# Six attention groups as one pipeline of 24 steps, with a new group order and a combine that is fed directly

## The chip, the cores and the metric

One Trainium2 chip, one of its cores. A core has five engines with queues of their own: TensorE (PE, with its weight loads shown apart as PEld), VectorE (DVE), ScalarE (ACT), GpSimd (POOL) and SyncE (SP), which in this kernel issues nearly all DMAs. The metric is device microseconds (us) of one launch, lower is better. Times are medians of runs; the profile is that of one more execution.

## The reference

One layer of a causal decoder trunk for 1024 prompt tokens and 32 sample tokens (8 sequences of 4), width 1024, all in float32:

```python
h = layer_norm(ALPHA * x + 0.5 * swiglu(x, f1_w1, f1_w3, f1_w2), ln1_g, ln1_b)
z = h @ w_in + b_in                       # q, k, v, uv, ga, gb
# attention: 3 groups of 4 heads of 64, (window, dilation) = (128,1), (512,4), (2048,16)
s = q @ k.T * SCALE + bias                # banded by window, positions split by dilation
m = max(s); p = exp(s - m); l = sum(p); o = (p @ v) / l; lse = m + log(l)
att = sum over the 3 groups of o * softmax(lse over the groups)
yb, vrows = sgu_branch(uv, ...)           # chunked causal gating
mix = (sigmoid(ga) * (att @ w_oa) + sigmoid(gb) * (yb @ w_ob)) @ w_out
h = layer_norm(ALPHA * h + mix, ln2_g, ln2_b)
h = layer_norm(ALPHA * h + 0.5 * swiglu(h, f2_w1, f2_w3, f2_w2), ln3_g, ln3_b)
```

The sample tokens attend to stored windows; the new windows are outputs too. The change is in the prompt's attention and in the weighting of its three groups.

## The kernel before, in words

Activations lie transposed: 128 features on the partitions, 1056 tokens (1024 prompt, 32 sample) along the free axis, in four chunks of 264. Float32 products are made of three matmuls on split operands (high part times high, high times low, low times high), line L240. The kernel runs through a first feed-forward stage, the projection `z` (`widen`, which writes each block of 128 rows of z to a DRAM tensor `zD`), the stage `mix`, and a second feed-forward stage. Everything below is in `mix`.

`mix` has a foreground of dense matmuls: the remaining gate blocks of z (`dense8`; they are stored to `zD` or kept), then 32 "locals" (`local`: eight blocks of 128 output rows by four chunks, twelve matmuls of `yb @ w_ob` each, whose result is multiplied into the gate tile `mt` on DVE, line L1544), then 32 products of `att @ w_oa` with six matmuls each (the same line L1544 after them), then the product with `w_out`. Each foreground piece ends with `tick`, which advances background generators: `bg` by 2 or 3 yields (`STEPS`), `slow` by 1, `mid` by 3. In `bg` stand six `attend` generators, one for each pair of head pair `hp` (0, 1) and group `g` (0, 1, 2), in the order `HPG` = (0,0), (0,1), (0,2), (1,0), (1,1), (1,2). In `mid` stand the gating branch (`sgu_norm`, `sgu_mix`) and the `combine` of a head pair; in `slow` the attention of the sample tokens (`sample`, which streams slabs `kv` from DRAM through the "M" tiles, line L1365) and `sample_join`.

One `attend` loads q, k, v (`fetch_z`, line L1138, 528 KB each) and the bias (L1165, L1172), transposes v to `V` (L1180) and makes four steps over pairs of query blocks. A step is `scores` (eight matmuls, L1200; then on DVE the bias and the row minimum, L1208, and on ACT the exponential with its row sum, L1212), `turn` (transposes of the probabilities, L1223, copied by ACT, L1227) and `values` (L1239, copied by ACT to the group's result `aT`, L1246 or L1250). The pipeline is filled and emptied in each group: in round t come `values(t-2)`, `turn(t-1)`, `scores(t)`. At its end the row minima and sums `ml` are transposed (L1263), copied (L1265) and stored to DRAM as `mlD` (L1267).

`combine(hp)` starts when all three groups of a head pair are done. It loads `mlD` back in the tokens' own order (`raw`, L1284, L1289), computes the three groups' weights with 16 partitions on DVE (L1298 to L1311) and one exponential on ACT, stores them as `cD` (L1313), loads each weight row broadcast over 64 partitions (`cbs`, L1318, three tiles), multiplies (L1323, L1325) and adds (L1326) into a new tile `att`. `held` allocates a tile and marks it with a copy by POOL (L108). `split_att` then splits `att` into high and low parts (L251 on ACT, L252 on DVE) for the product with `w_oa`.

All larger tiles come from one pool, "S", with 37 buffers: a load into a tile waits until the last reader of the buffer's former tile is done. PSUM has three "mm" tiles for the foreground and five "ax" tiles. The instructions of all generators are put into their final order by a list scheduler that works on its own estimates of durations; the order on each engine is then fixed, and a DMA that waits holds up those behind it on SP.

Of the kernel before, what the change touches and what calls it, by code (L numbers as in the profile page):

```python
# [21 lines left out]
P = 128  # L22
# [31 lines left out]
HPG = [(hp, g) for hp in range(2) for g in range(3)]  # L54
# [9 lines left out]
SPREAD = 2  # L64
# [17 lines left out]
class Trunk:  # L82
# [1000 lines left out]
    def widen(self):  # L1083
        nc, a = self.nc, self.a
        self.att = [None, None]
        self.attT = {}
# [67 lines left out]
    def attend(self, i):  # L1154
        nc, a = self.nc, self.a
        hp, g = HPG[i]
        w, dil = GROUPS[g]
        self.fetch_qkv(i)
        q, k, v = self.qkv.pop(i)
        bias = self.M([P, 2, 256])  # L1160
        bd = self.bD[g]
        if g < 2:
            for h in range(2):
                b = bd[2 * hp + h]
                nc.sync.dma_start(bias[:, h], bass.AP(b.tensor, b.offset + 127, [[383, P], [1, 256]]))  # L1165
        else:
            nc.vector.memset(bias[:, :, :P], BIG)
            for h in range(2):
                b = bd[2 * hp + h]
                for r in range(2):  # L1170
                    o = slice(64 * r, 64 * r + 64)
                    nc.sync.dma_start(bias[o, h, o], bass.AP(b.tensor, b.offset + 255, [[383, 64], [1, 64]]))  # L1172
        yield from self.pause(2 if i else 8)
        follower = i + 1
        V = self.Q([P, 8, P])
        for b in range(2):
            p = self.ax_tile()
            for i in range(4):
                j = 4 * b + i
                nc.tensor.transpose(p[:, i * P : (i + 1) * P], v[:, j * P : (j + 1) * P], self.ident)  # L1180
            nc.scalar.copy(V[:, 4 * b : 4 * b + 4], p.rearrange("p (i x) -> p i x", i=4))
            yield
        ml = self.X([P, 2, 2, 8], "ml")
        aT = self.S([P, NP])
        self.attT[hp, g] = aT
        prob, turned, pv = {}, {}, {}

        def span(i):
# [3 lines left out]
        def scores(t):  # L1192
            s = prob[t] = self.S([P, 2, 2, 256])
            pS = [self.ax_tile().rearrange("p (r k) -> p r k", r=2) for _ in range(2)]
            for r in range(2):
                i = 2 * t + r
                nk, k0, _ = span(i)
# [5 lines left out]
            for h in range(2):  # L1203
                for r in range(2):
                    i = 2 * t + r
                    nk, _, b0 = span(i)
# [9 lines left out]
        def turn(t):  # L1216
            s = prob.pop(t)
            pT = [self.ax_tile().rearrange("p (h k) -> p h k", h=2) for _ in range(2)]
            for r in (1, 0):
                for h in range(2):  # L1220
                    for b in range(span(2 * t + r)[0] // P):
                        o = slice(b * P, b * P + P)
                        nc.tensor.transpose(pT[r][:, h, o], s[:, r, h, o], self.ident)  # L1223
            sT = turned[t] = self.S([P, 2, 2, 256])
            for r in (1, 0):
                nk = span(2 * t + r)[0]
                nc.scalar.copy(sT[:, r, :, :nk], pT[r][:, :, :nk])  # L1227

        def values(t):
            sT = turned.pop(t)  # L1230
            if t % 2 == 0:
                pv[0] = self.ax_tile()
            for r in range(2):
                i = 2 * t + r
                nb = span(i)[0] // P
# [7 lines left out]
            if t % 2:  # L1243
# [3 lines left out]
                else:  # L1247
                    n = dil // 2
                    o = aT.rearrange("p (j r) -> p r j", r=dil)[:, n * b : n * b + n, :]
                    nc.scalar.copy(o, pv[0].rearrange("p (r j) -> p r j", r=n))  # L1250
# [12 lines left out]
        nc.tensor.transpose(pm, ml.rearrange("p m h i -> p (m h i)"), self.ident)  # L1263
        mt = self.X([32, P], "mt")
# [600 lines left out]
```

## Time and profile before

| | |
|---|---|
| median of three runs | 2182.03 us (2177.48 to 2182.41) |
| the profiled execution's own time | 2182.69 us |
| its span, first to last instruction | 2180.6 us |
| PE busy | 2129.5 us, 98% of the span |
| DVE, ACT busy | 1558.7 us (71%), 891.4 us (41%) |
| HBM | 304.34 MB read, 165.60 MB written, 216 GB/s over the span |
| granted TensorE clock, mean | 0.991 |
| part of the span with prompt attention on PE | 1072.6 to 1285.6 us |

The page gives busy times of engines and, for groups of instructions, the count, the mean duration and the idle time before them with what ended it. Times within the span are counted from its start. A row of the view of busy times by stretch has the stretch, its length, then busy time and count for PE, PEld, DVE, ACT and POOL, then the granted clock of TensorE (1.00 is full speed), the busy share of the DMA engines and GB/s.

### The profile page before, as it was taken

Reading aid. Unit: us, or ns where it says so; the run is one execution under the profiler, and the core shown is the slowest. Engines: PE = TensorE matmul, PEld = TensorE weight load, DVE = VectorE, ACT = ScalarE, POOL = GpSimd, SP = SyncE. Lnnn points to the kernel's source line nnn. Section 1 sums busy time; section 2 is a strip of 40 time slices with the busy share of each in tenths; the row PEclk is TensorE's granted clock in tenths of the full one; section 3 lists DMA queues with packets and bytes.
Section 4 is the critical chain, followed back from the end, with each engine's and each line's share of the span. In section 5 each row is a group of like instructions: output and inputs, shape, how many; then the busy total and the mean of one; then the engine's idle time right before and its main releaser. Section 6 shows DMA issues by size and latency. Waiting matters only on the chain.

```text
span 2180.6 us, 43243 instructions
## 1 busy us (share of the span) xinstructions
PE 2129.5 (98%) x17305; PEld 2090.8 (96%) x17305; DVE 1558.7 (71%) x2731; ACT 891.4 (41%) x1680; POOL 326.6 (15%) x247
## 2 busy tenths in 40 slices
PE   9999999999999999999999997999999999999997
PEld 8999999999998999999998897999999999999997
DVE  8776776656798725787666558778577677657886
ACT  5444444421124734334365553255444444421224
POOL 0432332200010012232000000000333233100000
PEclk9999999999999999999999999999999999999998
DMA  4445545698874335666855645414354554597842
GB/s 159 146 135 170 190 154 166 215 346 325 327 275 163 126 106 182 208 214 229 297 170 200 192 161 179 175 67 148 120 177 158 177 177 158 181 408 274 307 183 80
DMA packets 168569, 426.57 MB, mean 196 GB/s; under 512 B 24416, under 2 KB 59984, under 8 KB 165680
## 3 DMA queue, kind: packets, MB, share of 16 engines
q1 hardware_dynamic: 167936, 423.28, 55.3%
q8 instruction: 135, 2.21, 0.4%
q10 hardware_dynamic: 432, 0.54, 0.1%
q14 instruction: 66, 0.54, 0.1%
HBM read 304.34 MB, written 165.60 MB: 216 GB/s over the span
## 4 chain that ended last, share of the span: by engine, by line
PE 83%; DMA 7%; DVE 5%; ACT 2%; issue 1%; POOL 1%; SPq 0%; ACTq 0%; DVEq 0%; POOLq 0%
PE ax L240 45%; PE mm L240 35%; DMA S<-zD 2%; DMA M<-kv 1%; DMA R<-wz 1%; PE ax L1200 1%; PE ax L1239 1%; DVE W L252 1%; DVE S L252 1%; PE ax L1223 1%; DMA S<-hD 0%; DVE S L627 0%; DMA R<-wzp 0%; DVE S L1544 0%; ACT S L251 0%
## 5 line engine op out<-in xcount | busy, mean ns | idle before, releaser
L240 PE MATMUL mm<-S,W 128*128 128x264 f32 x5208 | 693.1, 288 | 22.1 <-DVE S L1544 9.9
L240 PE MATMUL ax<-S,W 128*128 128x264 f32 x5400 | 707.2, 284 | 1.1 <-ACT S L1030 0.9
L240 PEld LDWEIGHTS mm<-S,W 128*128 128x128 f32 x5208 | 657.1, 190 | 39.5 <-issue 11.8
L240 PEld LDWEIGHTS ax<-S,W 128*128 128x128 f32 x5400 | 676.7, 188 | 3.6 <-ACT S L1030 1.9
L240 PE MATMUL ax<-S,S 128*128 128x264 f32 x3240 | 476.9, 285 | 4.6 <-DVE S L1039 3.0
L240 PEld LDWEIGHTS ax<-S,S 128*128 128x128 f32 x3240 | 428.0, 188 | 6.1 <-DVE S L1039 4.4
L240 PE MATMUL mm<-S,S 128*128 128x264 f32 x2472 | 384.9, 286 | 2.6 <-DVE S L252 2.3
L240 PEld LDWEIGHTS mm<-S,S 128*128 128x128 f32 x2472 | 335.1, 189 | 4.3 <-DVE S L252 2.5
L251 ACT CAST W<-R 128x1024 fp32r<-128x1024 f32 (+3 forms) x173 | 128.5, 761 | 301.8 <-PE mm L240 136.4
L382 POOL TENSOR_TENSOR Q<-R 128x512 f32<-128x512 f32 x49 | 70.9, 1446 | 796.9 <-DMA R<-wz 180.9
L252 DVE TENSOR_TENSOR W<-R,W 128x1024 fp32r<-128x1024 f32 (+3 forms) x173 | 155.5, 902 | 22.8 <-ACT W L251 22.2
L251 ACT CAST W<-Q 128x1024 fp32r<-128x1024 f32 (+1 forms) x78 | 76.7, 984 | 223.3 <-DVE Q L383 89.2
L816 DVE SCALAR_TENSOR_TENSOR S<-ax,S 128x264 f32<-128x264 f32 x240 | 99.5, 427 | 67.7 <-PE ax L240 67.4
L457 DVE TENSOR_TENSOR S<-ax,M 128x264 f32<-128x264 f32 x82 | 32.7, 433 | 149.3 <-PE ax L240 144.4
L252 DVE TENSOR_TENSOR S<-Q,S 128x1024 fp32r<-128x1024 f32 (+1 forms) x78 | 111.1, 1424 | 4.1 <-ACT S L251 3.8
L252 DVE TENSOR_TENSOR W<-Q,W 128x1024 fp32r<-128x1024 f32 (+1 forms) x78 | 90.5, 1160 | 24.4 <-ACT W L251 24.4
L251 ACT CAST S<-Q 128x1024 fp32r<-128x1024 f32 (+1 forms) x78 | 76.7, 984 | 68.5 <-PE ax L240 50.1
L108 POOL CAST S<-ones 128x1 fp32r<-128x1 f32 x32 | 17.5, 567 | 490.3 <-PE mm L240 308.2
L251 ACT CAST S<-R 128x512 fp32r<-128x512 f32 (+1 forms) x64 | 44.0, 687 | 107.3 <-DMA sumsA<-S 40.4
L252 DVE TENSOR_TENSOR S<-S,M 128x528 fp32r<-128x528 f32 x72 | 84.5, 1173 | 3.0 <-ACT M L251 1.4
L383 POOL TENSOR_TENSOR Q<-Q,R 128x512 f32<-128x512 f32 x49 | 81.9, 1671 | 2.7
L390 POOL TENSOR_TENSOR Q<-R,Q 128x512 f32<-128x512 f32 x49 | 80.7, 1648 | 1.1
(207 smaller groups left out, 2050.2 us busy)
## 6 DMA issues: line engine op xcount, KB each, us to landing
ws<-st SPq DMA_DIRECT2D x144, 256.0 KB
S<-sumsA SPq DMA_DIRECT2D x63, 528.0 KB
S<-sumsB SPq DMA_DIRECT2D x63, 528.0 KB
M<-kv SPq DMA_DIRECT2D x96, 256.0 KB
sumsA<-M SPq DMA_DIRECT2D x90, 264.0 KB
sumsB<-M SPq DMA_DIRECT2D x90, 264.0 KB
R<-w13b SPq DMA_DIRECT2D x44, 512.0 KB
R<-w13a SPq DMA_DIRECT2D x42, 512.0 KB
```

The costliest lines, as they stand in the source:

```text
L108: self.nc.gpsimd.tensor_copy(t[:, 0, :1] if len(shape) == 3 else t[:, :1], self.ones[:, :1])
L240: mm = lambda a, b, s, e: nc.tensor.matmul(o, a[:, cc], b, start=s, stop=e, skip_group_check=True)
L251: a = self.nc.scalar.copy(hi, src)
L252: b = self.nc.vector.tensor_tensor(lo, src, hi.bitcast(F32), op=ALU.subtract)
L382: tt(s12[:, lo], cd[:, lo], cd[:, hi], op=ALU.add)
L383: tt(s12[:, hi], s12[:, lo], ab[:, lo], op=ALU.subtract)
L390: tt(s34[:, hi], ab[:, hi], s12[:, hi], op=ALU.subtract)
L457: go(one, 5, False, lambda x: tt(h[:, x, 1], one[x], p7[:, x], op=ALU.add))
L816: nc.vector.scalar_tensor_tensor(y(x, r, e), bank[x], HALF, y(x, r, e), op0=ALU.mult, op1=ALU.add)
L1200: nc.tensor.matmul(pS[h][:, r, :nk], q[e, i * P : (i + 1) * P], k[e, k0 : k0 + nk], start=True, stop=True)
L1223: nc.tensor.transpose(pT[r][:, h, o], s[:, r, h, o], self.ident)
L1239: nc.tensor.matmul(pv[0][e, (i % 4) * P : (i % 4 + 1) * P], V[:, i - (nb - 1) + b, e], sT[:, r, h, b * P : b * P + P], start=b == 0, stop= ...
```

## The change

`HPG` becomes (0,1), (0,2), (0,0), (1,1), (1,2), (1,0); the blocks of q, k and v are projected and the sample's pairs are formed in that order too. The six generators become one, with 24 steps that run through without emptying: round n holds `scores(n)` and `turn(n-1)`, then two yields, `values(n-2)`, two yields. In the third round of a group the next group's q, k, v are loaded, in its fourth round their v is transposed (`begin`). Biases are loaded for two groups at once into one "S" tile, before in "M" tiles.

The result `att` is built in group 0's own tile, which is why group 0 comes last: groups 1 and 2 store their minima and sums as before, but load them back as soon as group 2 is done (`sums`), while group 0's are transposed straight into the layout that `combine` uses, two transposes and one copy without DRAM. `combine` starts with the arithmetic; of the three broadcast weight tiles two are loaded at first and the third when the first multiply is issued. Group 0's multiply writes in place, where before it wrote a fourth tile. `sample_join` is put ahead of the column sums in `slow`.

```diff
-HPG = [(hp, g) for hp in range(2) for g in range(3)]
+HPG = [(hp, g) for hp in range(2) for g in (1, 2, 0)]
...
-        for t in range(6):
-            if t > 1:
-                values(t - 2)
-            if 0 < t < 5:
-                turn(t - 1)
-            if t < 4:
-                scores(t)
-            if t == 3:
-                self.fetch_qkv(follower)
-            yield from self.pause(SPREAD)
-        pm = self.ax_tile()[:32, :P]
-        nc.tensor.transpose(pm, ml.rearrange("p m h i -> p (m h i)"), self.ident)
-        mt = self.X([32, P], "mt")
-        nc.vector.tensor_copy(mt, pm)
-        D_ = self.mlD[hp, g]
-        nc.sync.dma_start(D_.rearrange("m h (i x) -> (m h i) x", x=P), mt)
-        yield
-        if g == 2:
-            self.mid.append(self.combine(hp))
-            if hp:
-                self.slow.append(self.sample_join())
+        def sums(i):
+            hp, g = HPG[i]
+            ml = open_.pop(i)[3]
+            if g:
+                pm = self.ax_tile()[:32, :P]
+                nc.tensor.transpose(pm, ml.rearrange("p m h i -> p (m h i)"), self.ident)
+                mt = self.X([32, P], "mt")
+                nc.vector.tensor_copy(mt, pm)
+                nc.sync.dma_start(self.mlD[hp, g].rearrange("m h (i x) -> (m h i) x", x=P), mt)
+                if g == 1:
+                    return
+                raw = self.held([P, 3 * 2 * P])[:16].rearrange("p (g m x) -> p g m x", g=3, m=2)
+                self.raw[hp] = raw
+                for g in (1, 2):
...
+            else:
+                pm = self.ax_tile()[:16, : 2 * P].rearrange("p (m x) -> p m x", m=2)
+                for m in range(2):
+                    nc.tensor.transpose(pm[:, m], ml[:, m].rearrange("p h i -> p (h i)"), self.ident)
+                nc.vector.tensor_copy(self.raw[hp][:, 0], pm)
+                self.mid.append(self.combine(hp))
...
+        N = 4 * len(HPG)
+        for n in range(N + 2 + 1):
+            i, t = divmod(n, 4)
+            if n < N:
+                scores(n)
+            if 0 <= n - 1 < N:
+                turn(n - 1)
+            if t == 2 and i < len(HPG):
+                self.fetch_qkv(i + 1)
+                if i % 2:
+                    biases.update((x, load_bias(x)) for x in range(i + 1, min(i + 3, len(HPG))))
+            yield from self.pause(2)
+            if 0 <= n - 2 < N:
+                values(n - 2)
+                if (n - 2) % 4 == 3:
+                    sums((n - 2) // 4)
+            if t == 3 and i + 1 < len(HPG):
+                begin(i + 1)
+            yield from self.pause(2)
...
     def combine(self, hp):
-        att, *cbs = [slot([P, NT]) for _ in range(4)]
...
+        load(0)
+        load(1)
         yield from self.pause(3)
-        for g, cb in enumerate(cbs):
-            cb, aT = cb[:, :NP], self.attT.pop((hp, g))
-            if g == 0:
-                nc.vector.tensor_tensor(att[:, :NP], aT, cb, op=ALU.mult)
-            else:
-                nc.vector.tensor_tensor(aT, aT, cb, op=ALU.mult)
+        for g in range(3):
+            aT = self.attT.pop((hp, g))
+            load(g + 2)
+            nc.vector.tensor_tensor(aT, aT, cbs.popleft(), op=ALU.mult)
+            if g:
                 nc.vector.tensor_tensor(att[:, :NP], att[:, :NP], aT, op=ALU.add)
```

Since every instruction's place comes from the scheduler, the order on each engine moves. Two places follow, first before and then after; line numbers of the changed kernel are its own.

SP, the DMA queue, around the loads of q, k, v of (1,1), the blocks `zD_8631`, `zD_8637` and `zD_8643` (before L1138, after L1137). Before:

```order
L212 DMA ws<-st 16x4096 x2
L1365 DMA M_13150<-kv 128x512
L1172 DMA M_14900<-bD 64x64 x4
L1365 DMA M_13151<-kv 128x512
L1365 DMA M_13149<-kv 128x512
L1365 DMA M_13150<-kv 128x512
L1138 DMA S_14372<-zD_8631 128x1056
L1138 DMA S_14374<-zD_8637 128x1056
L1138 DMA S_14376<-zD_8643 128x1056
```

After (L1269 stores `mlD`, L1278 loads it back, L1623 stores a gate block, L218 loads a weight block, and L1137 of `zD_8648` is a tile of the gating branch):

```order
L1398 DMA M_13108<-kv 128x512
L1269 DMA mlD<-X_13813 32x128
L1137 DMA S_13848<-zD_8648 128x1056
L1278 DMA S_13816<-mlD 8x16x8 x4
L1137 DMA S_13912<-zD_8631 128x1056
L1623 DMA zD_8656<-W_13857 256x1x264
L1137 DMA S_13914<-zD_8637 128x1056
L1137 DMA S_13916<-zD_8643 128x1056
L218 DMA R_14470<-wzp 128x1024
```

Three slab loads and four bias loads no longer stand right ahead of these loads; a store and four loads of `mlD` do.

DVE, the end of `combine(1)` (multiplies L1323 and L1325 before, L1357 after; adds L1326, now L1359; the split of `att` L252, now L251; the locals' multiplies L1544, now L1577). Before:

```order
L1323 TENSOR_TENSOR S_15243<-S_14195,S_15245 128x1024
L1544 TENSOR_TENSOR S_15388<-S_15388,mm_15809 128x264
L1325 TENSOR_TENSOR S_14631<-S_14631,S_15247 128x1024
L1544 TENSOR_TENSOR S_15388<-S_15388,mm_15823 128x264
L1325 TENSOR_TENSOR S_14955<-S_14955,S_15249 128x1024
L1544 TENSOR_TENSOR S_15388<-S_15388,mm_15837 128x264
L1326 TENSOR_TENSOR S_15243<-S_15243,S_14631 128x1024
L252 TENSOR_TENSOR W_15876<-R_15875,W_15876 128x256
L1326 TENSOR_TENSOR S_15243<-S_15243,S_14955 128x1024
L252 TENSOR_TENSOR S_15870<-S_15243,S_15869 128x32
L252 TENSOR_TENSOR S_15870<-S_15243,S_15869 128x1024
L1544 TENSOR_TENSOR S_15857<-S_15857,mm_15884 128x264
```

After:

```order
L1357 TENSOR_TENSOR S_14717<-S_14717,S_15322 128x1024
L251 TENSOR_TENSOR W_15577<-R_15576,W_15577 128x512
L1577 TENSOR_TENSOR S_15228<-S_15228,mm_15582 128x264
L1466 COPY S_13968<-ax_15596 64x32 x2
L1466 COPY S_15059<-ax_15596 64x32 x2
L1359 TENSOR_TENSOR S_15059<-S_15059,S_14717 128x1024
L1577 TENSOR_TENSOR S_15228<-S_15228,mm_15606 128x264
L251 TENSOR_TENSOR S_15849<-S_13968,S_15848 128x32
L1577 TENSOR_TENSOR S_15228<-S_15228,mm_15620 128x264
L251 TENSOR_TENSOR S_15855<-S_15059,S_15854 128x32
L1577 TENSOR_TENSOR S_15228<-S_15228,mm_15634 128x264
L251 TENSOR_TENSOR S_15855<-S_15059,S_15854 128x1024
```

Before, the last local's multiply (`mm_15837`) stands ahead of the last add, and the first product with `w_oa` (`mm_15884`) right behind the split; after, the split's last row has 12 more locals' multiplies behind it (`mm_15654` to `mm_15822`) before the first product with `w_oa` (`mm_15869`).

More of the change, by code (lines that the diff above doesn't have):

```diff
@@ L63 @@
 MID = 3
-SPREAD = 2
 HOP = (4, 1, 4)
@@ L1294, in combine @@
-        yield
+        raw = self.raw.pop(hp)
+        t = [raw[:, g] for g in range(3)]
         nat = lambda g, x: x.rearrange("p (r b) -> p b r", r=GROUPS[g][1])
@@ L1563, in mix @@
         self.mid.extend(sgu)
-        self.bg.extend(self.attend(i) for i in range(len(HPG)))
-        kept, end = {}, NLEAD + NTAIL - LAST
+        self.bg.append(self.attend())
+        self.sums, kept, end = None, {}, NLEAD + NTAIL - LAST
         units = {NLEAD: self.unit(a["wzp"][NLEAD])}
```

162 lines of the change are left out of this document (86 added, 76 removed).

## The prediction

> **What bounds the kernel now.** I read the page first: PE is busy nearly all the time, so a change in the attention can only win what PE loses around it, and it can lose at most as much again as it makes PE wait.
>
> ```profile
> PE 2129.5 (98%) x17305; PEld 2090.8 (96%) x17305; DVE 1558.7 (71%) x2731; ACT 891.4 (41%) x1680; POOL 326.6 (15%) x247
> ```
>
> Busy times by stretch of the stage with the attention show where PE loses (columns: stretch, length, busy time and count of PE, PEld, DVE, ACT, POOL, then granted clock, DMA share, GB/s):
>
> ```profile
> 1060.00:1140.00 80.00, 79.46 (x677) 72.93 (x677) 55.77 (x158) 49.40 (x120) 0.00 (x0) 1.00 0.66 220
> 1140.00:1220.00 80.00, 78.56 (x661) 70.15 (x659) 55.54 (x164) 45.32 (x131) 1.47 (x8) 1.00 0.64 211
> 1220.00:1236.00 16.00, 12.26 (x64) 10.06 (x62) 6.70 (x23) 6.73 (x18) 0.00 (x0) 0.68 0.25 84
> 1284.00:1288.00 4.00, 1.77 (x18) 1.25 (x16) 1.04 (x4) 1.66 (x3) 0.00 (x0) 1.00 1.00 387
> 1288.00:1316.00 28.00, 27.80 (x229) 27.59 (x228) 20.69 (x56) 12.66 (x17) 0.00 (x0) 1.00 0.65 222
> 1316.00:1336.00 20.00, 11.55 (x67) 10.22 (x65) 12.88 (x19) 4.22 (x5) 0.00 (x0) 0.74 0.64 176
> 1336.00:1380.00 44.00, 40.56 (x317) 38.82 (x315) 39.27 (x62) 20.12 (x25) 1.42 (x3) 1.00 0.63 217
> ```
>
> For 160 us of attention PE is idle 0.54 + 1.44 us. Then three places: 3.74 us at 1220, 2.23 us at 1284, 8.45 us at 1316. The first and last also have a clock below 1.00. By four microseconds:
>
> ```profile
> 1224.00:1228.00 4.00, 4.00 (x22) 3.02 (x24) 1.28 (x6) 1.67 (x4) 0.00 (x0) 0.57 0.11 11
> 1228.00:1232.00 4.00, 4.00 (x21) 3.02 (x18) 1.86 (x10) 2.18 (x8) 0.00 (x0) 0.50 0.05 7
> 1232.00:1236.00 4.00, 4.00 (x24) 4.00 (x24) 3.28 (x8) 0.91 (x2) 0.00 (x0) 0.65 0.00 0
> 1320.00:1324.00 4.00, 0.83 (x4) 0.65 (x5) 2.99 (x4) 0.00 (x0) 0.00 (x0) 0.95 1.03 235
> 1324.00:1328.00 4.00, 1.83 (x6) 1.21 (x6) 3.60 (x5) 0.00 (x0) 0.00 (x0) 0.50 0.37 149
> 1328.00:1332.00 4.00, 2.01 (x7) 1.71 (x8) 2.04 (x4) 2.33 (x2) 0.00 (x0) 0.50 0.71 234
> 1332.00:1336.00 4.00, 4.00 (x28) 3.99 (x26) 3.98 (x7) 1.49 (x2) 0.00 (x0) 0.77 0.16 31
> ```
>
> After the first wait PE works 12 us at 0.57, 0.50 and 0.65, which loses 4.00 x (0.43 + 0.50 + 0.35) = 5.1 us. In the last it loses 0.83 x 0.05 + 1.83 x 0.50 + 2.01 x 0.50 + 4.00 x 0.23 = 2.9 us. After the 2.23 us the next stretch shows 1.00. So the three places cost 3.74 + 5.1 = **8.8**, **2.2**, and 8.45 + 2.9 = **11.3** us: 22.4 us in all. That is what the change can win; the other losses of the stage are near 2 us before 1220 and 3.44 us after 1336.
>
> Who ends these waits, by the view of PE's waits from 1060 to 1380 (us in total, times, longest):
>
> ```profile
> PE mm L240 <- DVE S L1544: 9.9, 9, 2.7
> PE ax L1180 <- DMA S<-zD: 3.7, 1, 3.7
> PE mm L240 <- ACT S L251: 2.7, 1, 2.7
> ```
>
> **The first place: the load of v.** The timeline has SP's issues and PE:
>
> ```profile
> 1211.98 1.04 PE L1223 MATMUL ax<-ident,S 128*128 128x128 f32 x8
> 1212.50 3.76 SPq L1365 DMA_DIRECT2D M<-kv  x3
> 1216.31 1.37 SPq L1138 DMA_DIRECT2D S<-zD  x3
> 1223.98 1.44 PE L1180 MATMUL ax<-ident,S 128*128 128x128 f32 x8 [3.74 <-DMA S<-zD]
> ```
>
> The loads of q, k, v of (1,1) wait for buffers that the transposes at 1211.98 free, but leave SP only at 1216.31, behind three slab loads that waited for DVE. PE reaches v's transposes before it has landed. The changed order has no slab there; a store of `mlD`, one tile of the gating branch and loads of `mlD` stand ahead instead. By the waits in the order, v of (1,1), (1,2) and (1,0) now wait for PE instructions that stand 54, 46 and 49 dense matmuls and 18 to 24 small ones ahead of v's transposes. The rates:
>
> ```profile
> 745.40 46.32 PE mm L240 x382
> 1212.14 0.87 PE ax L1223 x8
> ```
>
> A dense matmul is 46.32 / 382 = 0.121 us, a small one at most 0.87 / 8 = 0.11 us, so the covers are 54 x 0.121 + 19 x 0.11 = 8.6, 46 x 0.121 + 24 x 0.11 = 8.2 and 49 x 0.121 + 18 x 0.11 = 7.9 us. A load of before stood just so: v of (1,0) had 35 dense and 36 small matmuls, 8.2 us, and did not stall:
>
> ```profile
> 1172.26 7.68 SPq L1138 DMA_DIRECT2D S<-zD  x4
> 1178.95 0.60 PE L1223 MATMUL ax<-ident,S 128*128 128x128 f32 x4
> 1185.60 0.66 PE L1180 MATMUL ax<-ident,S 128*128 128x128 f32 x4
> ```
>
> It waited for the transposes at 1178.95, and the transposes at 1185.60 carry no wait. So I let the 8.8 us go. What is late next is one of the three loads: from nothing to a stall like the old one, 8.8 us, each. I take 1.5 us for all three, since their cover is that of the load that came in time, with other traffic around it.
>
> For the price of such a stall the Trainium skill (TensorE: Matmul & The Clock Gate, "Part 1: The HAM clock gate") has a rule: an idle window of about 3.4 us halves the clock, and about 3.4 us of sustained work restores it. The trace agrees with the drop (3.74 us does it, 2.23 us does not) and not with the return, which takes 12 us here; by the page the first place would cost 3.7 + 3.4 x 0.5 = 5.4 us and the whole sum would be 3.4 us smaller. I go by the rows.
>
> **The second place** is a gate tile loaded too late for a local:
>
> ```profile
> 1286.96 1.11 DVE L1544 TENSOR_TENSOR S<-S,mm 128x264 f32<-128x264 f32 x3 [5.65 <-DMA S<-zD]
> ```
>
> In the new order the gate tiles' buffers are free more than 100 dense matmuls ahead of their use, over 12 us at 0.121. The 2.2 us go; what hides the load is the tail of the attention, and without it the 2.2 us would be back.
>
> **The last place: combine(1).** Its chain in the timeline, from the last attention matmuls to the first full row of products with `w_oa`:
>
> ```profile
> 1284.97 0.66 PE L1239 MATMUL ax<-S,Q 128*64 128x128 f32 x8 [0.41 <-ACT S L1227]
> 1288.29 0.32 SPq L1267 DMA_DIRECT2D mlD<-X  x1
> 1296.45 1.74 SPq L1289 DMA_DIRECT2D S<-mlD  x4
> 1303.03 0.40 DVE L1300 TENSOR_TENSOR X<-X,S 16x128 f32<-16x128 f32 x1
> 1311.22 0.89 DVE L1311 TENSOR_TENSOR S<-X,S 16x128 f32<-16x128 f32 x3
> 1319.86 1.23 DVE L1323 TENSOR_TENSOR S<-S,S 128x1024 f32<-128x1024 f32 x1 [3.73 <-DMA S<-cD]
> 1331.02 5.17 PE L240 MATMUL mm<-S,W 128*128 128x264 f32 x30 [0.23 <-DVE S L252]
> ```
>
> 1285.6 to 1331.0 is 45.4 us: 17.4 us until the second minimum on DVE (a store and loads of `mlD`), 9.1 us of arithmetic, 7.75 us for `cD` there and back, 11.2 us of multiplies, adds and the split. As cover the order has 253 dense matmuls, 30.7 us. The difference, 14.7 us, is about what the second and last places show. Now group 0's sums need no DRAM, and groups 1 and 2 are stored and loaded while group 0 still runs. That leaves 9.1 + 7.75 + 11.2 = 28 us and a copy. The order has 372 dense matmuls behind the last attention instruction, 45.0 us, because the attention ends ten locals earlier. The spare is 17 us: the 11.3 us go.
>
> What is late next is DVE's own queue. The first multiply waits for `cD` on DVE (3.73 us in its row above), and locals' multiplies stand behind it, each of which frees one of three PSUM tiles. Between the last weight (L1337) and the first multiply stand four locals, 4 x 12 x 0.121 = 5.8 us against 7.75: DVE waits some 2 us, and the sample's join, which now stores and loads its result among these locals, adds to it. PE runs up to three locals ahead, 4.4 us. I take 1.5 us, between 0 and 5 (the whole 3.73 and a second such wait of over a microsecond).
>
> **The steps themselves.** The matmuls are the same but for two transposes more, 0.2 us. The new order crowds the last four steps, those of (1,0). ACT's rows:
>
> ```profile
> L1212 ACT ACTIVATE S<-S,X 128x256 f32<-128x256 f32 x44 | 21.9, 499 | 10.4 <-DVE X L1208 10.3
> L1227 ACT COPY S<-ax 128x512 f32<-128x512 f32 x22 | 12.4, 587 | 12.2 <-PE ax L1223 12.2
> L1250 ACT COPY S<-ax 128x512 f32<-128x512 f32 x8 | 8.5, 1068 | 4.3 <-PE ax L1239 4.2
> L1572 ACT ACTIVATE S<-mm,cols 128x264 f32<-128x264 f32 x12 | 5.5, 481 | 8.5 <-PE mm L240 8.5
> ```
>
> A step of full width takes ACT 4 x 0.50 + 2 x 0.59 + 1.07 / 2 = 3.7 us, four of them with three gate copies of 0.48 us 16.2 us. On PE stand 72 dense and 82 small matmuls from the first scores of step 20 to the values of step 22: at most 8.7 + 9.0 = 17.7 us. That is level; I take 1.0 us, from 0 to 3. A tile of the gating branch is now loaded among the attention steps and waited for by DVE; such a wait stood in the old kernel too, and cost PE nothing:
>
> ```profile
>   DVE M L1523: 3.4, 1
> ```
>
> I take 0.5 us, from 0 to 3. Biases in "S" instead of "M", the one multiply in place and the reordered projection before 1060 cost nothing or change sign by chance: the same instructions stand there, and the stalls of that stage follow the sample's slabs, which are as many. Bounds 1 us either way.
>
> **The sum** against the profiled execution's 2182.69 us: -8.8 - 2.2 - 11.3 + 1.5 + 1.5 + 0.2 + 1.0 + 0.5 = -17.6, so 2165.1 us. That execution was 0.7 us above the median of the runs (2182.03); I say **2165 us**. With all new costs at 0 it is 2159.6; I let 2157 be the low end, for the 2 us still lost before 1220. With them at the ends other than the loads (5 + 3 + 3 + 1) it is 2173.
>
> **Rivals.**
> (1) One load of v is late. Against it is the old load with the same cover; for it, that a store waiting for DVE stands ahead of the first. 8.8 in place of 1.5: 2172.4 us. Chance 0.15.
> (2) The last place stays: the join's store and loads hold SP, `cD` leaves late and DVE blocks while PE has three tiles. It would take more than the 17 us of spare for the split to be late, but locals on DVE can stall by themselves. 11.3 in place of 1.5: 2175 us. Chance 0.10.
> (3) The clock falls in the crowded tail, where PE does mostly transposes and small matmuls. Rows of the old kernel with such work show 1.00 (1060 to 1220 above), in shorter runs. The tail's 17 us at half clock would cost 8.5 us: 2173.6. Chance 0.05. The Trainium skill speaks for it (TensorE: Matmul & The Clock Gate, "Part 4: PE-mode transpose"): transposes do not count as busy time for the clock gate. By that rule the sum would be 8.5 us smaller.
> (4) Slower: the pipeline asks for q, k, v only when the third round is reached, and all three loads of v, or two of them and a weight tile of `combine(0)`, miss their cover by as much as the old one did. Three stalls with the clock behind them are 3 x 8.8 = 26.4 in place of 1.5 us: 2190. It decides from 11 us between a buffer coming free and v's landing; the old case with SP held up had 12. Chance 0.15.
>
> My forecast, all three places gone with small new costs, has 0.55. Differences within 0.3% (6.5 us, so from 2175.5 to 2188.6) are about what a measurement of this kernel cannot tell from no change. The forecast lies wholly below it; of (1) 0.09, of (2) 0.04, of (3) 0.03: faster 0.71. Same: 0.06 + 0.06 + 0.02 + 0.02 of (4), 0.16. Slower: 0.13 of (4). The range to 2184 leaves out most of (4) and the ends below 2157, under 0.2.
>
> **What would show it.** Right: no wait of PE for `zD` above 1 us; no stretch of clock below 0.9 between the attention's start and the products with `w_oa`; at the first of these products DVE has done the split some ten locals before. Wrong: a row "PE ax <- DMA S<-zD" of 3 us with half clock behind it (1, 4), idle time of PE that a local's multiply ends during `combine(1)` of 5 us or more (2), or half clock in the last four steps without an idle time ahead (3).

## The result, and the profile after

| | before | after |
|---|---|---|
| median of six runs each | 2181.79 us | 2166.80 us (2162.63 to 2168.50) |
| ratio of after to before | | 0.9931, 95% interval 0.9918 to 0.9944 |
| the profiled execution's own time | 2182.69 us | 2166.30 us |
| its span | 2180.6 us | 2164.2 us |

The change makes the kernel 15.0 us faster; forecast were 16.8 (2165 us, 2157 to 2184). The page after, first part:

```profile
PE 2126.6 (98%) x17307; PEld 2087.7 (96%) x17307; DVE 1551.9 (72%) x2727; ACT 889.0 (41%) x1680; POOL 325.2 (15%) x245
```

The busy times by stretch of the stage, with columns as before:

```profile
1070.00:1140.00 70.00, 69.38 (x589) 61.67 (x587) 46.39 (x153) 48.95 (x135) 0.50 (x1) 1.00 0.68 232
1140.00:1212.00 72.00, 72.00 (x602) 63.91 (x603) 48.99 (x146) 41.72 (x118) 1.63 (x5) 1.00 0.59 182
1212.00:1236.00 24.00, 22.34 (x183) 19.42 (x182) 17.76 (x56) 13.44 (x45) 0.58 (x1) 1.00 0.88 285
1236.00:1280.00 44.00, 44.00 (x360) 39.08 (x359) 20.74 (x64) 25.63 (x57) 0.74 (x4) 1.00 0.42 134
1280.00:1300.00 20.00, 17.00 (x133) 16.11 (x132) 14.83 (x35) 3.54 (x7) 0.00 (x0) 1.00 0.78 232
1300.00:1320.00 20.00, 20.00 (x166) 19.99 (x166) 12.32 (x24) 4.21 (x6) 0.00 (x0) 1.00 0.50 138
1320.00:1332.00 12.00, 9.84 (x64) 9.23 (x63) 10.23 (x17) 5.12 (x8) 0.00 (x0) 0.86 0.53 178
1332.00:1364.00 32.00, 31.07 (x245) 29.92 (x244) 27.84 (x43) 15.00 (x18) 1.43 (x3) 1.00 0.64 214
```

The idle times of 3.74, 2.23 and 8.45 us are gone, and with them the 8.0 us of low clock behind the first and the last. What PE still loses here: 1.66 us from 1212 to 1236, 3.00 from 1280 to 1300, and 2.16 from 1320 to 1332, at a clock of 0.86. Who ends these waits (us in total, times, longest):

```profile
PE mm L239 <- DVE S L1577: 4.1, 6, 1.5
PE ax L1225 <- ACT S L1229: 1.0, 1, 1.0
PE ax L1184 <- DMA S<-zD: 0.7, 1, 0.7
```

The wait for v has shrunk from 3.7 to 0.7 us. The chain of `combine(1)`, in the timeline from the transposes of group 0's sums to the end of the split:

```profile
1264.70 0.39 PE L1285 MATMUL ax<-ident,X 128*16 128x128 f32 x2
1266.30 0.37 DVE L1326 TENSOR_TENSOR X<-S 16x128 f32<-16x128 f32 x1
1277.57 0.89 DVE L1337 TENSOR_TENSOR S<-X,S 16x128 f32<-16x128 f32 x3
1286.55 1.22 DVE L1357 TENSOR_TENSOR S<-S,S 128x1024 f32<-128x1024 f32 x1 [3.27 <-DMA S<-cD]
1297.50 1.22 DVE L251 TENSOR_TENSOR S<-S,S 128x1024 fp32r<-128x1024 f32 x1
1313.14 0.43 DVE L1577 TENSOR_TENSOR S<-S,mm 128x264 f32<-128x264 f32 x1 [1.01 <-PE mm L239]
1314.62 0.43 DVE L1577 TENSOR_TENSOR S<-S,mm 128x264 f32<-128x264 f32 x1 [1.05 <-PE mm L239]
1315.40 0.42 DVE L1577 TENSOR_TENSOR S<-S,mm 128x264 f32<-128x264 f32 x1
```

From 1265.09 (the end of the first row) to 1298.72 (the end of `L251`, the split's last row) it takes 33.6 us. The multiplies L1577 come 1.48 us apart as long as they follow locals of twelve matmuls, and then 0.78 us apart: the first product with `w_oa` begins near 1314.6, so 15.9 us were to spare.

One thing stands here that the prediction did not have. The scores on PE, by line and form (count, busy time, mean ns of one), of before and then of after:

```profile
L1200 PE MATMUL ax<-S,S 64*128 64x256 f32 x88 | 15.0, 403 | 0.0
L1200 PE MATMUL ax<-S,S 64*128 64x128 f32 x104 | 12.4, 314 | 0.0
```

```profile
L1201 PE MATMUL ax<-S,S 64*128 64x256 f32 x88 | 18.5, 391 | 0.0
L1201 PE MATMUL ax<-S,S 64*128 64x128 f32 x104 | 12.6, 307 | 0.0
```

Each matmul is no longer than before (391 against 403 ns), yet together they cover 31.1 us against 27.4, of which 1.4 us were the low clock of the first place (two groups of four at 1225.35 and 1228.83 took 1.57 us each, where such a group takes 0.86 at full speed). The timeline of the last steps, after:

```profile
1237.17 1.13 PE L1201 MATMUL ax<-S,S 64*128 64x256 f32 x4
1238.55 1.13 PE L1201 MATMUL ax<-S,S 64*128 64x256 f32 x4
```

These are the two heads of one step, four matmuls each, with dense matmuls between them: 1.13 us for each head. Where a step's eight matmuls stand side by side, all eight take 1.14 us (a row with the experiments). The heads use rows 0 to 63 and 64 to 127 of the array and overlap when they are neighbours. The Trainium skill (TensorE: Matmul & The Clock Gate, "Part 3: Packing small matmuls — row/col tiling") says that matmuls on tiles of different rows run at the same time, and this trace agrees; the experiments give the price of losing it.

### The profile page after: what moved, and what is told of

It is laid out like the page before. It is cut to its first block, busy times and chain, and to the rows that moved or that the text cites. A ratio compares the mean times of both kernels' runs of the same rounds, so it can differ in the third digit from the quotient of the medians.

```text
span 2164.2 us, 43247 instructions
## 1 busy us (share of the span) xinstructions
PE 2126.6 (98%) x17307; PEld 2087.7 (96%) x17307; DVE 1551.9 (72%) x2727; ACT 889.0 (41%) x1680; POOL 325.2 (15%) x245
## 4 chain that ended last, share of the span: by engine, by line
PE 89%; DVE 5%; DMA 4%; ACT 1%; issue 1%; POOL 0%; SPq 0%; ACTq 0%; DVEq 0%; POOLq 0%
PE ax L239 47%; PE mm L239 38%; PE ax L1201 1%; DMA S<-zD 1%; PE ax L1248 1%; PE ax L1225 1%; DVE W L251 1%; DVE S L251 1%; DMA S<-cD 0%; DMA M<-kv 0%; DVE S L1577 0%; DMA R<-wz 0%; DVE S L626 0%; DMA R<-w2a 0%; PE ax L1543 0%
## 5 line engine op out<-in xcount | busy, mean ns | idle before, releaser
L239 PE MATMUL mm<-S,W 128*128 128x264 f32 x5208 | 693.5, 287 | 13.6 <-DVE S L1577 4.1
L251 DVE TENSOR_TENSOR W<-R,W 128x1024 fp32r<-128x1024 f32 (+3 forms) x173 | 156.5, 908 | 23.9 <-ACT W L250 22.9
L251 DVE TENSOR_TENSOR S<-Q,S 128x1024 fp32r<-128x1024 f32 (+1 forms) x78 | 108.5, 1391 | 3.8 <-ACT S L250 3.8
L251 DVE TENSOR_TENSOR W<-Q,W 128x1024 fp32r<-128x1024 f32 (+1 forms) x78 | 89.9, 1153 | 27.2 <-ACT W L250 27.2
L251 DVE TENSOR_TENSOR S<-S,M 128x528 fp32r<-128x528 f32 x72 | 84.5, 1174 | 2.6 <-ACT M L250 0.8
```

The costliest lines, as they stand in the source:

```text
L239: mm = lambda a, b, s, e: nc.tensor.matmul(o, a[:, cc], b, start=s, stop=e, skip_group_check=True)
L251: b = self.nc.vector.tensor_tensor(lo, src, hi.bitcast(F32), op=ALU.subtract)
```

## The experiments

Runs were compared with the kernel before on the same chip, so each has a ratio. A second measure leaves out what happens ahead of the attention. The two matmuls on `ones` at the start of the attention stand in the same place in all these kernels, and the time at which they start differs from execution to execution even for the same code:

```profile
1073.12 1.02 PE L1453 MATMUL ax<-S,ones 128*128 128x512 f32 x2
```

```profile
1070.31 1.02 PE L1486 MATMUL ax<-S,ones 128*128 128x512 f32 x2
```

```profile
1076.80 1.02 PE L1486 MATMUL ax<-S,ones 128*128 128x512 f32 x2
```

The second and third are the changed kernel, 6.5 us apart. The last column is the span less that start. It comes from one execution of each kernel, and for the changed kernel's two it is 1093.9 and 1091.0, so a difference of under 3 us in it says nothing; below, each kernel is compared with both.

| kernel | edit | median, us | ratio to before, 95% | from `ones` to the end |
|---|---|---|---|---|
| before | | 2181.79 | 1 | 1107.5 |
| after | the change | 2166.80 | 0.9931 (0.9918 to 0.9944) | 1093.9 |
| again | the change, second time | 2169.92 | 0.9936 (0.9913 to 0.9959) | 1091.0 |
| widen | old projection order | 2169.29 | 0.9944 (0.9925 to 0.9962) | 1094.0 |
| together | heads side by side | 2163.22 | 0.9919 (0.9893 to 0.9946) | 1089.8 |
| apart | heads apart | 2177.82 | 0.9993 (0.9975 to 1.0010) | 1103.8 |
| bearly | before, earlier loads | 2183.51 | 1.0013 (0.9995 to 1.0031) | 1106.7 |
| late | later loads | 2173.04 | 0.9970 (0.9956 to 0.9984) | 1097.4 |
| trip | group 0 by DRAM | 2168.91 | 0.9946 (0.9929 to 0.9963) | 1094.4 |
| slowend | attention's end spread out | 2174.19 | 0.9970 (0.9957 to 0.9983) | 1098.2 |
| pool | combine on GpSimd | 2173.00 | 0.9969 (0.9952 to 0.9985) | 1099.6 |
| both | together and pool | 2168.17 | 0.9948 (0.9928 to 0.9968) | 1094.9 |
| defer | together, multiplies later | 2164.10 | 0.9929 (0.9911 to 0.9947) | 1089.9 |
| slab4 | defer and a fourth slab tile | 2159.53 | 0.9894 (0.9872 to 0.9916) | 1087.8 |

**together** keeps the heads' matmuls neighbours:

```diff
+            m = nc.vector.memset(pS[0][:, 0, :1], 0.0).ins
+            with self.tc.issue_after(m):
+                nc.vector.memset(pS[1][:, 0, :1], 0.0)
...
-                    nc.tensor.matmul(
+                    with self.tc.issue_after(last) if last else ExitStack():
+                        last = nc.tensor.matmul(
```

> The changed kernel with the four scores matmuls of a step kept side by side on PE, the two heads in turn (each PSUM tile is first marked by a small DVE memset, so that both are there before the first matmul). Theory A: matmuls of the two heads, which use different halves of the rows, overlap when they stand side by side, and the change lost that in seven steps; in its trace a step of 256 wide blocks takes 1.06 us for each head apart against 1.06 us for both together, a mixed one 0.85, a narrow one 0.64: 4 x 1.06 + 2 x 0.85 + 0.64 = 6.6 us. So 2166.8 - 6.6 = 2160 us, and the busy time of the 64x256 scores on PE falls from 18.5 to 15 us. Rival B: the lost overlap costs nothing, since PE fills the stage otherwise, or the marks on DVE hold up the steps by as much: 2165 to 2169 us.

**apart** puts the second head's two matmuls behind the turn of the step before:

```diff
-                for h in (1, 0):
+            for h in (1, 0):
+                if h == 0 and 0 <= n - 1:
+                    turn(n - 1)
...
+                with self.tc.issue_after(turns[n - 1]) if h == 0 and n else ExitStack():
```

> The changed kernel with the two heads' scores set apart in all steps but the first: the second head's matmuls stand behind the turn of the step before. Theory A (the overlap of the heads is lost): 9 mixed steps x 0.85 + 6 wide x 1.06 + 8 narrow x 0.64 = 19.1 us against 6.6 in the changed kernel: 12.5 us more, 2179 us, without new idle time on PE of over 3 us. Rival B (the overlap is worth nothing): 2167 us, or slower only by idle time that the view of PE's waits names (the exponentials or the turn's copies).

The scores by line and form, together and then apart, and a step of together in the timeline:

```profile
L1206 PE MATMUL ax<-S,S 64*128 64x256 f32 x88 | 12.8, 391 | 0.0
L1206 PE MATMUL ax<-S,S 64*128 64x128 f32 x104 | 10.6, 307 | 0.0
```

```profile
L1204 PE MATMUL ax<-S,S 64*128 64x256 f32 x88 | 24.8, 391 | 0.0
L1204 PE MATMUL ax<-S,S 64*128 64x128 f32 x104 | 20.6, 307 | 0.0
```

```profile
1246.52 1.14 PE L1206 MATMUL ax<-S,S 64*128 64x256 f32 x8
```

The same 192 matmuls cover 23.4 us as neighbours and 45.4 us apart; after has 31.1, so the change lost 7.7 us to this where before lost some 2.6 (27.4 - 1.4 - 23.4). These are busy times by form, which count what the matmuls overlap with others; the 6.6 us of together's expectation leave that out. The kernel apart takes 14.3 us more of PE than after and is 10 to 13 us slower from `ones` to the end, though PE idles less (0.62 us from 1070 to 1290, for 3.77 in after): theory A, and its rival is out. The kernel together won only 1 to 4 us in that measure, less than its theory A said, and its trace names a reason:

```profile
1213.71 1.23 DVE L1362 TENSOR_TENSOR S<-S,S 128x1024 f32<-128x1024 f32 x1 [2.79 <-DMA S<-cD]
1218.26 0.28 DVE L1214 CUSTOM_DVE_ANT_0 S<-ax,S 128x128 f32<-128x128 f32 x1
1219.58 0.69 PE L1230 MATMUL ax<-ident,S 128*128 128x128 f32 x2 [2.91 <-ACT S L1218]
```

The first multiply of `combine(0)` waits on DVE for its weights in `cD`, and the reductions of a step whose scores ended at 1210.66 stand behind it until 1218.26. PE then waits 2.91 us for the exponentials, and the clock is 0.67 from 1220 to 1224. So of the 7.7 us won on PE, 2.91 + 4 x 0.33 = 4.2 went there; in after, by the chain of waits, the same multiply cost 0.96 us.

**bearly** and **late** move the loads of q, k and v by a round, in the kernel before and in the changed one:

```diff
# bearly
-            if t == 3:
+            if t == 2:
                 self.fetch_qkv(follower)
# late
-            if t == 2 and i < len(HPG):
+            if t == 3 and i < len(HPG):
                 self.fetch_qkv(i + 1)
```

> The kernel before with one edit: q, k, v of the next group are asked for in the third round instead of the fourth. Theory A (the first place is SP's queue alone): the wait of PE for v at 1220 and the low clock behind it go, 8.8 us of 2181.8: 2173 us, the other two places stay. Rival B: the slabs still hold the queue or the buffers come no earlier: a wait for zD of over 2 us stays and the time is 2179 to 2183 us.

> The changed kernel with the next group's q, k, v asked for in the fourth round of a group instead of the third; the transposes of v stay where they are. Theory A (what removed the first place is the cover of the loads, some 8 us, of which a load takes 7.65 us from the free buffer to landing in the changed kernel's trace): a round of cover less leaves 1 to 3 us, so each of the loads in a running pipeline is late by 4 to 7 us and the clock falls behind some of them: 15 to 35 us slower than the changed kernel, 2182 to 2202 us, with rows PE <- DMA S<-zD of 3 us and more. Rival B (the loads are early enough anyway, the first place went because the slabs no longer stand ahead of them): within 2 us of the changed kernel.

Both theories A fell, and neither rival came whole. In bearly no wait for `zD` by the transposes of v is left, but the time is that of before. Two other waits came, each with a low clock behind it:

```profile
1158.29 0.71 PE L1200 MATMUL ax<-S,S 64*128 64x128 f32 x4 [1.49 <-ACT S L1250]
1243.45 1.23 DVE L1323 TENSOR_TENSOR S<-S,S 128x1024 f32<-128x1024 f32 x1 [4.40 <-DMA S<-cD]
1250.75 0.87 PE L1223 MATMUL ax<-ident,S 128*128 128x128 f32 x6 [2.88 <-ACT S L1212]
```

The first is scores that wait for a copy of ACT. The second is again DVE waiting for `cD` (4.40 us, and 2.27 more at 1246.95) in front of a step's reductions; in before the same multiply waited 2.68 us, at 1241.95, and PE did not wait behind it. Idle time and low clock of the two come to 1.49 + 2.88 us and some 3.3 + 1.5 us, 9.2 us, about the 8.8 that went. With the loads on time, other waits are what the attention runs into; the edit also moves the scheduler's order, so one run does not show that any such edit would meet them. In late the waits for v are 1.9 us in all, 1.4 the longest, and to the 3.5 to 6.4 us that it is slower from `ones` to the end they give 1.2; 1.5 us are scores that wait for DVE, and 2.4 us heads apart (33.5 us of scores). So a round of cover is worth 1 to 2 us in the changed kernel. What keeps the first place away there is then probably that no slabs stand ahead of the loads (in late three loads leave SP at 1203.50 with three slabs behind them); that was not tried by itself.

**trip** sends group 0's sums through DRAM as well (`if g:` is always true, and the loads run over all three groups), and **slowend** takes the cover away:

```diff
-            yield from self.pause(2)
+            yield from self.pause(6 if n >= 20 else 2)
```

> The changed kernel with group 0's sums also stored to DRAM and loaded back with those of groups 1 and 2, as in the kernel before; everything else as changed. Theory A (the longer cover is what removed the last place): the chain gets some 16 us longer, from 33.6 us to about 50 from the last attention matmul to the end of the split, against 372 dense matmuls, 45.0 us, and 3 us of idle time that are there already: 2 to 4 us slower than the changed kernel. Rival B (the direct path was what removed it): the 11.3 us of the last place are back in full, 2178 us. Rival C: still hidden, within 1.5 us.

> The changed kernel with the last four steps of the attention spread out (six yields for two), so that only 108 dense matmuls, 13.1 us, stand behind the last attention matmul as cover for combine(1), in place of 372, 45.0 us. Theory A (the last place is the chain against its cover): the chain takes 33.6 us in the changed kernel, so PE waits for some 33.6 - 13.1 = 20 us, and 2 to 4 us more at a low clock behind it: 2166.8 + 22 = 2189 us. Rival B (the last place went because of the direct path or the third weight tile): within 4 us of the changed kernel.

In trip the chain from the last attention matmul to the end of the split is 38.5 us (1262.65 to 1301.19), against 34.0 us in after (1264.76 to 1298.72): 4.6 us longer and not 16, since eight of the twelve loads of `mlD` were issued ahead and four were left. The split still ends 13.9 us before the first product with `w_oa`, and the time is that of rival C: its ratio is 0.0010 above the changed kernel's on the same chip, less than either interval reaches to one side. Its trace is less kind than its time:

```profile
1288.00 1.23 DVE L1352 TENSOR_TENSOR S<-S,S 128x1024 f32<-128x1024 f32 x1 [4.77 <-DMA S<-cD]
1289.62 7.17 PE L239 MATMUL mm<-S,W 128*128 128x264 f32 x36 [3.24 <-DVE S L1572]
```

DVE waits longer for `cD` (4.77 us for 3.27), PE behind it 3.24 us, and the clock is 0.56 and 0.59 from 1288 to 1296. From 1280 to 1300 PE loses 3.70 us idle and 2.69 by the clock, for 3.00 in after. The 3.4 us more do not show in the total: fewer heads are apart (29.3 us of scores for 31.1), and the low clock at the first products with `w_oa` did not come. So the direct path is not what removed the last place, but it may be worth some 3 us.

In slowend PE waits where the old kernel did:

```profile
1314.28 0.63 PE L239 MATMUL mm<-S,W 128*128 128x264 f32 x3 [2.48 <-DVE S L1577]
1317.07 0.45 PE L1463 MATMUL ax<-ident,X 128*128 128x128 f32 x1 [2.16 <-DVE X L1460]
1322.41 1.03 PE L239 MATMUL mm<-S,W 128*128 128x264 f32 x3 [4.89 <-ACT S L250]
```

That is 9.5 us of idle time, and the clock is 0.50 from 1316 to 1328: theory A in kind. The time from `ones` is 4 to 7 us longer, not 22: the chain is shorter when DVE has few locals in between, 25.7 us from 1297.93 to 1323.62, against some 14 us of dense matmuls (the 14.12 us from 1297.68), and the spread-out steps keep more heads together (28.1 us of scores for 31.1). So the cover is what removed the last place.

**widen** gives the projection and the sample's pairs the old group order (a second list of pairs, used there), and **again** is the changed kernel unedited.

> The changed kernel with the projection of q, k, v and the sample's pairs in the old group order, the attention unchanged. Theory A: 3.2 us of the gain were made ahead of 1060 us by the new order of the projection; they go back: 2170 us, and PE's idle time from 880 to 1060 us rises from 4.65 to about 6.5 us. Rival B: that difference between the two profiles is chance of the schedule: within 1.5 us of 2166.8.

> The changed kernel itself, unedited, to stand beside the other three. By the first measurement 0.9931 of the kernel before, 2166.8 us; with another chip of the day some us apart from that in the absolute.

Both profiles start the attention later than after's by more than before stands from after, so the 2.8 us between the latter two can be chance of the execution. Theory A's other sign did come: PE idles 6.3 us from 880 to 1060 in widen, 6.6 in before and 4.65 in after. But bearly, with the old order, has 5.1 and trip, with the new one, 5.9, so this too is within the spread; widen does not decide between its theories. From `ones` to the end widen is like the changed kernel.

**pool** (on after) and **both** (on together) move the combine's multiplies and adds (`nc.vector` to `nc.gpsimd` in those two calls); **defer** leaves them on DVE but behind more of its other work; **slab4** adds a tile to that.

> The changed kernel with the three multiplies and two adds of each combine on GpSimd instead of DVE. Theory A: what is left of the last place is DVE waiting for the weights in cD with other work queued behind it (3.27 us at 1286 in the changed kernel's trace, 3.0 us of PE idle from 1284 to 1300, and 0.96 us at 1213 for combine(0)); on GpSimd nothing is queued behind that wait: 4 us less than the changed kernel, 0.9913 of before, 2163 us. The split comes later by about 6 us (GpSimd is slower), inside the spare of some 14 us. Rival B: those idle times belong to the sample's join and to the gate tiles: within 1.5 us of the changed kernel.

> The changed kernel with both edits: heads side by side, and the combine's multiplies and adds on GpSimd. Theory A: the heads side by side saved 6.6 us on PE but only 3 to 4 us in the end, because a step's reductions stood on DVE behind the first multiply of combine(0), which waited 2.79 us for its weights (PE idle 2.91 us, then the clock at 0.67 for 4 us); with that multiply off DVE the two gains add up: 6.6 + 4 us less than the changed kernel, 2156 us, 0.988 of before. Rival B: the 6.6 us are partly taken up by something else (the turn waits for the exponentials anyway): 2160 to 2163 us.

> The kernel with the heads side by side (together), and the multiplies of both combines kept on DVE but put later: combine(0)'s behind the reductions of two more steps, combine(1)'s behind 7 locals more after the weights. Theory A: DVE waiting for cD with the steps' reductions or locals queued behind it costs 2.91 us at 1219 with 1.3 us of clock, and 1.23 + 0.84 us at 1290, in the trace of together; these 6 us go: 0.989 of before, 2157 us. Rival B: DVE then waits for the sample's slabs in the same place instead (as it did for 4.51 us when the multiplies stood on GpSimd), and the time stays that of together, 0.992 of before.

> The kernel defer (heads side by side, the combine's multiplies later) with a fourth tile for the sample's slabs. In defer DVE waited 4.71 us for a slab at 1207 with the next steps' reductions queued behind it, PE idled 3.27 us and lost some 3 us more at a clock of 0.50 and 0.78. Theory A: the slab is late because its load waits for one of three tiles; with four it is asked for earlier and that place goes: 6 us less than defer, 0.990 of before, 2158 us. Rival B: the slab is late because the DMA engines are full there with the weights from cD (share 0.98 to 1.02 from 1208 to 1216 in the changed kernel), so it lands no earlier: within 2 us of defer, 0.993 of before.

```diff
# defer
-        yield from self.pause(3)
+        yield from self.pause(54 if hp else 12)
...
-            nc.vector.tensor_tensor(aT, aT, cbs.popleft(), op=ALU.mult)
+            with self.tc.issue_after(self.done if hp else self.reduced):
+                nc.vector.tensor_tensor(aT, aT, cbs.popleft(), op=ALU.mult)
# slab4, besides
-SLABS = 3
+SLABS = 4
```

(`done` is the last local's multiply, `reduced` the last reduction of a step so far.) In pool, `both` and defer theory A fell, and DVE's wait for a slab has a part in each; the timeline of `both` and then of defer:

```profile
1209.72 4.67 POOL L1362 TENSOR_TENSOR S<-S,S 128x1024 f32<-128x1024 f32 x2 [3.60 <-DMA S<-cD]
1212.42 2.52 DVE L1429 TENSOR_TENSOR M<-M,X 128x512 f32<-128x512 f32 x1 [4.51 <-DMA M<-kv]
1216.12 0.69 PE L1230 MATMUL ax<-ident,S 128*128 128x128 f32 x2 [4.59 <-ACT S L1218]
```

```profile
1211.45 1.36 DVE L1430 TENSOR_TENSOR M<-M,X 128x512 f32<-128x512 f32 x2 [4.71 <-DMA M<-kv]
1215.59 1.23 PE L1206 MATMUL ax<-S,S 64*128 64x128 f32 x8 [3.27 <-DVE ax L1198]
```

With the multiplies out of the way, DVE waits in the same place for a slab of the sample, 4.51 and 4.71 us, and the steps' reductions stand behind that (in defer also the small memset ahead of the next step, line L1198, for which PE waits 3.27 us). In defer that is rival B, with its time. In pool the slab costs DVE 3.20 us, and GpSimd's multiplies hold DVE up besides (last section): PE's longest wait there, 3.38 us at 1223.44, stands behind both. With a fourth slab tile, in slab4, the wait on DVE's timeline is 2.51 us, 5 us later, and the steps behind it cost PE less than 1 us: theory A.

```profile
1216.34 0.69 DVE L1430 TENSOR_TENSOR M<-M,X 128x512 f32<-128x512 f32 x1 [2.51 <-DMA M<-kv]
```

slab4 is the fastest of all, 0.9894 of before. From `ones` to the end it gains 3 to 6 us on the changed kernel; its interval ends at 0.9916, below the changed kernel's first (from 0.9918) and touching its second (from 0.9913). Against defer, from which it differs by the tile alone, the gain is 7.6 us by the ratios, whose intervals just overlap, and 2.1 us from `ones` to the end: the wait is shown to go, the size of the gain is not.

## Why the prediction was right

- **The three places.** 8.8, 2.2 and 11.3 us went as forecast, on the rows of the waits and the clock. For the last place the reason held: cover of 45.0 us against a chain of "28 us and a copy" left 17 us to spare; the chain measured 33.6, the spare 15.9, and slowend brought the wait back by taking the cover away. It is the earlier end of the attention that does it; without the direct path of group 0's sums (trip) the last place does not come back, though DVE's wait for `cD` costs more. For the first place the loads came nearly in time, 0.7 us for 1.5. But the prediction took that place as a loss by itself, and bearly shows that it isn't: removing it alone gained nothing, since the attention met two other waits, one for ACT and one behind DVE on `cD`. The second place went, and no run tested it by itself.
- **DVE's own queue**, 1.5 us (0 to 5): 3.0 us from 1280 to 1300, with DVE waiting 3.27 us for `cD` at 1286.55. Right in kind, half of its size. `combine(0)`'s wait in the middle of the attention was not in the sum; it cost 0.96 us.
- **"The matmuls are the same but for two transposes more, 0.2 us"** is the step that failed: the same matmuls in another order cost some 5 us more (7.7 lost for 2.6), because the heads of a step were separated. The pieces of order quoted ahead were of SP and DVE; PE's own order had this in it.
- **The crowded last steps**, 1.0 us, and the sgu's tiles, 0.5 us: PE has no idle time from 1236 to 1280, and the transposes L1501, which wait for a tile of the gating branch, lose 0.6 us, 0.1 more than in before (L1468, 0.5). Both about nothing. Rival (3) did not come either: the clock is 1.00 through the last steps. Dense matmuls stand between the small ones there, so a long run of transposes alone is not shown.
- **The sum.** -22.3 us, with 0.7 for v, 3.0 for DVE, 0.96 for `combine(0)`, 5.1 for the heads and 0.1 for L1501, is -12.4. The profiles give -13.6 and -16.5 from `ones` to the end (after, again), the medians -15.0. The losses that the prediction left alone changed both ways: the 2.0 us ahead of the first place are 0.62 now (1070 to 1212), while the products with `w_oa` lose 2.16 and 0.93 us and some 1.4 by the clock of 0.86, where before lost 3.44. The new costs were 9.9 us where the forecast had 4.7; that the total came within 2 us of it is partly luck, the spread of the executions.
- **Rivals (1), (2) and (4)** did not come: no load of v stalls PE by 3 us, no local's multiply holds it for 5 (4.1 us in all, 1.5 the longest), and late shows that even a round less of cover costs little.

## What to carry to other kernels

Removing a wait on the critical engine may win less than its length, because it can hide the next one: before summing such waits, find the next one in each place. Here it was mostly DVE's queue, which works in order and had three kinds of instructions in it that wait for DMA. Count not only the instructions of the critical engine but which of them are neighbours: here pairs on different rows of the array overlapped only then, and the scheduler, which did not know it, parted seven of 24. Compare profiles from a point just ahead of the place in question, and take a second execution of the same code to see the spread.

## What the runs showed of the hardware

**Neighbours on different rows.** Eight matmuls of 64 rows by 256 columns took 1.14 us side by side, and 1.13 us for each four when the two heads' fours stood apart.

**The clock does not follow the length of one idle time.** In bearly 1.49 us of idle time at 1156.80 was enough for half clock; in the kernel `both` 2.67 us ahead of 1304.28 were not. By four microseconds, bearly, then of `both` the row in the timeline and the stretch behind it:

```profile
1156.00:1160.00 4.00, 2.51 (x17) 1.94 (x15) 2.81 (x6) 3.08 (x6) 0.00 (x0) 0.92 0.33 127
1160.00:1164.00 4.00, 4.00 (x18) 3.78 (x18) 3.57 (x12) 3.03 (x12) 0.00 (x0) 0.50 0.10 11
1164.00:1168.00 4.00, 4.00 (x27) 4.00 (x27) 0.70 (x2) 0.48 (x1) 0.00 (x0) 0.73 0.56 192
```

```profile
1304.28 16.40 PE L239 MATMUL mm<-S,W 128*128 128x264 f32 x132 [2.67 <-DVE S L1582]
```

```profile
1304.00:1308.00 4.00, 3.72 (x30) 3.72 (x31) 3.40 (x7) 1.54 (x2) 0.00 (x0) 1.00 0.38 116
```

The same code does either: in the first products with `w_oa` the waits of after (0.56, 1.15 and 0.46 us) are followed by a low clock, and those of again (0.54, 1.14 and 0.46) are not. The stretches are after's, then again's:

```profile
1324.00:1328.00 4.00, 2.93 (x15) 2.71 (x16) 4.00 (x8) 1.53 (x3) 0.00 (x0) 0.79 0.33 130
1328.00:1332.00 4.00, 2.39 (x18) 2.16 (x18) 4.00 (x6) 2.09 (x3) 0.00 (x0) 1.00 0.43 171
```

The clock's own record in these traces has only full and half speed, so a value between them is a mean. Up to the kernel's end, a stretch at half lasts 3.41 us or two, three or four times that: 6.83 us here in bearly, 3.41 in after, 10.24 at each of before's two places (the prediction read 12 from its rows). The Trainium skill (TensorE: Matmul & The Clock Gate, "Part 1: The HAM clock gate") says that its window runs freely, so that the phase decides; that fits a longer idle time without and a shorter one with a fall, but 1.49 us is less than half of the 3.4 us that it gives for one idle window. The kind of work around the wait may count too: in bearly small matmuls stand among the dense ones before and behind it, in `both` dense ones alone. No run separates this from the phase.

**GpSimd and DVE get in each other's way.** In the kernel `both`, a multiply of 128x512 with two SBUF inputs took 2.52 us on DVE beside GpSimd's multiplies, and 0.68 alone. The rows shown with the experiments tell how: GpSimd's two multiplies end at 1214.39 (1209.72 + 4.67) and DVE's at 1214.94, 0.55 us later. The next pair does the same, with ends at 1217.41 and 1217.96:

```profile
1215.06 2.35 POOL L1364 TENSOR_TENSOR S<-S,S 128x1024 f32<-128x1024 f32 x1
1215.71 2.25 DVE L1429 TENSOR_TENSOR M<-M,X 128x512 f32<-128x512 f32 x1
```

Two more in pool end 0.54 and 0.55 us after GpSimd's. So DVE's multiply was not slowed by a factor but waited for GpSimd's to end. The reductions of a step, which read PSUM and SBUF, took their usual 0.28 us beside GpSimd's multiply at 1215.06. The Trainium skill (GPSIMD Engine Reference, "1. Specifications") names this case, DVE with two SBUF inputs, without a size; here it was the rest of GpSimd's instruction.
